# Third quarter's output gates as a Strassen pair inside attention, first value group inside the first long-convolution quarter

## The chip, the cores and the metric

The kernel runs on one core of one Trainium2 chip. The time is the device time of one execution in microseconds; the median over executions is compared. TensorE (PE), VectorE (DVE), ScalarE (ACT), GpSimd (POOL) and SyncE (SP) run side by side; each works through its own list of instructions in order, and semaphores tie the lists together.

## The reference, cut to what matters

One layer of a hybrid network for 640 tokens (128 context tokens and 512 latent tokens), width 1024, in fp32:

```
z = h @ w_in                                   # hy (3 x 1024), g_h, q, k, v, g_a, m
hy = short_conv(hy, conv_w, conv_b)            # 3 taps along the sequence
v_h, x1, x0 = split(hy)
u = v_h * x1
y_h = (irfft(rfft(u) * rfft(filter)) + u * d) * x0      # long convolution
y_a = attention(q, k, v)                       # neighbourhood attention, context keys
p_h = (y_h * silu(g_h)) @ w_bh
p_a = (y_a * silu(g_a)) @ w_ba
out = (sigmoid(m_h) * p_h + sigmoid(m_a) * p_a) @ w_out
x = layer_norm(alpha * x + gate * out)
```

The change concerns two parts of `z`: the output gates `g_h` of the long convolution, `y_h * silu(g_h)`, and the values `v` of attention.

## The kernel before, in words

All products are made of three passes: the operands are split into a high and a low part (`split`: ScalarE rounds the high part, line 112, VectorE subtracts, line 113), and high x high, high x low and low x high are summed. A weight tile is 128 x 1024; a projection (`proj`, matmuls on line 181) takes 8 slices x 3 passes x 2 halves of 320 columns, 48 matmuls. In the convolution quarters the low part of the weights is made by an accumulating transfer on GpSimd (line 161) instead of VectorE.

The kernel goes through these parts:

- A prologue (modulation, filters' hidden layers), with an order written out by hand.
- Four quarters of 256 channels of the long convolution. In quarter `q`, `quarter_head(q + 1)` projects and convolves `u` and `x1` of the next quarter and `quarter_tail(q)` projects `x0`; beside them run `gated_conv(q - 1)`, `long_conv(q)`, `long_conv_back(q)` (Fourier transforms as matmuls, with long chains of elementwise work on VectorE between them) and `filter_spectrum(q + 1)`. The function `weave` interleaves the two lists in the program; the compiler's scheduler then sets the order on every engine.
- `hand_over`, woven with the last quarter's convolution: `quarter_tail(3)`, then the value groups and the first queries and keys (`values(1)`, `values(2)`, `values(3)`, `queries(0)`, `keys(0)`, `values(0)`) with sums of the activations that the pairs below need (`early_sums`). A value group is 120 matmuls of 256 columns (lines 954 and 966) for 256 of the 1024 channels; groups 1 to 3 are stored to DRAM (`v_d`) and read back when attention comes to them (`values_back`). `attention_setup` closes the convolution's memory and opens attention's; `late_sums` make the remaining sums in it.
- Eight main stages of attention, in which TensorE's order is written out by hand: the attention steps of stage `j` (`attend(j)`) are woven into two or three pairs (`mains(j)`). A pair (`pair_tile`, matmuls on line 1229) computes two projection tiles with Strassen's scheme (Winograd's form): 7 products of 4 slices x 3 passes, 84 matmuls of 320 columns instead of 96; VectorE makes four sums of the weights (line 1189) and seven splits for it and combines the products (lines 1238 and 1244). The list `runs` names the order of the pairs, so that `prepare` can sum and split the next pair's weights while the present one runs.
- Output projections, again as plain tiles and pairs, and the layer norm.

The gates of a quarter in `LATE_GATES` are not computed in `quarter_tail`: `x0` alone is, in a compact layout; `gated_conv` stores `x0 * y` to DRAM (`yu_d`), and `gates_h(q)` in a main stage reads it back, computes the gates of both tiles as a pair, multiplies and stores the rows to `yh_d`. For a quarter that isn't listed, `quarter_tail` computes two plain gate tiles (`gate_tile`: one projection, tanh on ScalarE, two products on VectorE, line 571), GpSimd multiplies with `x0` (`gapped_product`), and `gated_conv` stores the finished rows. Before the change this is so for the third quarter (index 2) only. All rows of `yh_d` are read back around the end of the last main stage (`yh_raw`).

The list `GATED_AT` holds sixteen pairs in which, at the fourth product, one row of the output gate's modulation is added up on VectorE (`gate_row`, line 1338; 1024 columns). `EARLY_VALUES` maps a quarter to a value group that is computed at the end of that quarter's list; before the change it is empty. Such a group leaves its accumulators to the tile `dinv` in the convolution's memory, which the short convolution's taps use too. The projections, the values and the pairs share four PSUM banks (`ps_mm`); a projection takes two of them, a value group three.

Of the kernel before, what the change touches and what calls it, by code (L numbers as in the profile page):

```python
# [19 lines left out]
NK = 8  # L20
# [12 lines left out]

T_GH, T_Q, T_K, T_V, T_GA, T_MH, T_MA, T_BH, T_BA, T_WO = 24, 32, 40, 48, 56, 64, 72, 80, 88, 96

LATE_GATES = (0, 1, 3)
EARLY_VALUES = {}

PACKS = (
    (("cc", 16), ("bss", 16), ("sel", 2)),  # L40
# [10 lines left out]
def tile_hyena_natten_step(ctx: ExitStack, tc: tile.TileContext, a, o):  # L51
# [546 lines left out]
    def quarter_tail(q):  # L598
        for i in range(2):
            n = 2 * q + i  # L600
            if q in LATE_GATES:
                x0 = row(yhp, "yh", f"x0_{n}")
# [116 lines left out]
    def gated_conv(q):  # L719
# [7 lines left out]
        for i in range(2):  # L727
# [4 lines left out]
            for j, r in enumerate((0, 2, 1, 3)):  # L732
                nc.tensor.transpose(oy[:, r * P : r * P + P], ye[:, j, i * P : i * P + P], ident)
            if q in LATE_GATES:
                x0, s0 = out["yh"][n], SC
# [11 lines left out]
            for d in range(2):  # L747
                nc.vector.tensor_tensor(ys[:, :, 1:, d], x_rest[:, :, :, d], yo[:, :, :7, d], op=ALU.mult)
            nc.sync.dma_start((yu_d if q in LATE_GATES else yh_d)[n], yh[:])
            yield  # L750

    N_CONV, N_BACK, N_GATED = 10, 7, 2
# [10 lines left out]
    def chain(*gens):  # L763
        for g in gens:
            yield from g
# [56 lines left out]
    def early_sums():  # L822
        t = []
        yield from first_sums(0, t)
        yield from second_sum(0, t[0])
        yield from first_sums(1, t)
        out["early_sums"] = True
# [7 lines left out]
    def alongside(main, side, every, first=0):  # L835
        for i, _ in enumerate(main):
            if i >= first and i % every == 0:
                next(side, None)
            yield
        for _ in side:  # L840
            pass
# [50 lines left out]
    def queries(j):  # L892
        for hf, p in enumerate((yield from proj(T_Q + j, eng="dma", low_last=True))):
            q_half(j, hf, p[:, :HALF])
        yield
# [29 lines left out]
    def keys(j):  # L925
        cached_keys(j)
        for hf, p in enumerate((yield from proj(T_K + j, eng="dma", low_last=True))):
            k_half(j, hf, p[:, :HALF])
        yield

    def values(m):
        w = [wtile(T_V + 2 * m + i, "dma", width=256) for i in range(2)]
        ps = [acc(f"v{m}_{i}") for i in range(2)]
        if m:
            if m in EARLY_VALUES.values():
                v = hwa.tile([P, 1280], F32, tag="dinv", name=f"vs{m}")
                v = [v[:, 512 * i : min(512 * i + 512, 1280)] for i in range(3)]
            else:
                v = [slot(0, t, f"v{m}{t}")[:, :n] for t, n in (("k", 512), ("kl", 768))]
                v = [v[0], v[1][:, :512], v[1][:, 512:]]  # L940
        else:
            out["v0"] = slot(0, "v", "v0")
            v = [out["v0"][:, 512 * i : min(512 * i + 512, 1280)] for i in range(3)]

        def passes(k):
            wh, wl = w[k // 4][0][k % 4], w[k // 4][1][k % 4]
            return ((hH, wh, k == 0, False), (hL, wh, False, False), (hH, wl, False, k == NK - 1))

        for half in range(2):
            ks = range(4 * half, 4 * half + 4)  # L950
            for k in ks:
                for x, wk, first, last in passes(k):
                    for t in range(4):
                        nc.tensor.matmul(  # L954
                            ps[t // 2][:, t % 2 * 256 : t % 2 * 256 + 256], x[:, k, P * t : P * t + P], wk,
                            start=first and t % 2 == 0, stop=last, skip_group_check=True,
                        )
                yield
            if half:
                for i in range(2):  # L960
                    nc.scalar.activation(v[i], ps[i][:], AF.Copy)
            else:
                pe = acc(f"ve{m}")
            for k in ks:
                for x, wk, first, last in passes(k):
                    nc.tensor.matmul(pe[:, :256], x[:, k, P * 4 :], wk, start=first, stop=last, skip_group_check=True)  # L966
            yield
        nc.scalar.activation(v[2], pe[:, :256], AF.Copy)
        nc.sync.dma_start(o["new_v"][:, m * 256 : m * 256 + 256], v[0][:, :256])
        for i in range(3 if m else 0):  # L970
            nc.sync.dma_start(v_d[m][:, 512 * i : min(512 * i + 512, 1280)], v[i])
        yield
# [5 lines left out]
    N_VALUES = 11  # L978

    def early_values(q):  # L980
        if q in EARLY_VALUES:
            yield from values(EARLY_VALUES[q])

# [5 lines left out]
    def hand_over():  # L989
        nonlocal tp  # L990
        yield from quarter_tail(3)
        hwa_stack.close()
        out["slots_l"] = left.enter_context(tc.tile_pool(name="slots_l", bufs=1))
        out["slots_q"] = left.enter_context(tc.tile_pool(name="slots_q", bufs=1))
        tp = left.enter_context(tc.tile_pool(name="tp", bufs=1))
        yield from alongside(chain(values(1), values(2), values(3), queries(0), keys(0), values(0)), early_sums(), 1)

    tail = ctx.enter_context(ExitStack())
    ac = ctx.enter_context(ExitStack())
# [255 lines left out]
    def queries_keys(j):  # L1255
        cached_keys(j)
        yield from pair_tile(T_Q + j, T_K + j, lambda i, hf, src: k_half(j, hf, src, False) if i else q_half(j, hf, src))
# [12 lines left out]
    def gates_h(m):  # L1270
        yu = [row(yhp, "yh", f"yv{m}"), sp.tile([P, NT], F32, tag="yu", name=f"yw{m}")]
        for i in range(2):
            load_to(yu[i][:], yu_d[2 * m + i])

        def use(i, hf, src):
            th = sp.tile([P, HALF], F32, tag="c", bufs=4, name=f"tg{m}")[:]
            y = yu[i][:, CS[hf]]
            nc.scalar.activation(th, src, AF.Tanh, scale=0.5)
            nc.vector.tensor_tensor(y, y, src, op=ALU.mult)
            gate(th, y, y)  # L1280
            nc.scalar.dma_start(yh_d[2 * m + i][:, CS[hf]], y)

        yield from pair_tile(T_GH + 2 * m, T_GH + 2 * m + 1, use)

    def mix(m):
        t0, dst = (T_MH, mh_d) if m < 4 else (T_MA, ma_d)
        n0 = 2 * (m % 4)

        def use(i, hf, src):
            th = sp.tile([P, HALF], F32, tag="c", bufs=4, name=f"th{m}")[:] if hf == i == 0 else src  # L1290
            nc.scalar.activation(th, src, AF.Tanh, scale=0.5)
            nc.scalar.dma_start(dst[n0 + i][:, CS[hf]], th)

        yield from pair_tile(t0 + n0, t0 + n0 + 1, use)

    N_PAIR = 14

    def qk_(j):
        return T_Q + j, T_K + j

    def ga_(j):
        return T_GA + j, T_GA + j + 1

    def gh_(m):
        return T_GH + 2 * m, T_GH + 2 * m + 1

    def mix_(m):
        t = (T_MH if m < 4 else T_MA) + 2 * (m % 4)
        return t, t + 1

    runs = (
        (
            qk_(1), ga_(0), qk_(2), mix_(0), gh_(0), qk_(3), mix_(1), ga_(2), qk_(4), mix_(2), gh_(1), qk_(5), mix_(3), ga_(4), qk_(6), mix_(4), gh_(3), qk_(7), mix_(5), ga_(6), mix_(6), mix_(7),
        ),
    )
    follow = {x: y for run in runs for x, y in zip(run, run[1:])}
    GATED_AT = [runs[0][i][0] for i in (2, 3, 6, 7, 8, 9, 11, 12, 13, 14, 15, 17, 18, 19, 20, 21)]

    weave(hand_over(), chain(gated_conv(2), long_conv(3), long_conv_back(3), gated_conv(3), attention_setup(), late_sums()),
          2 * NK + 3 * N_VALUES + 16, 2 * N_GATED + N_CONV + N_BACK + 7)  # L1320
    gp = left.enter_context(tc.tile_pool(name="gp", bufs=1))
    gbc = gp.tile([P, 2, D], F32, tag="gbc", name="gbc")

# [49 lines left out]
    def last_pair(main):  # L1373
        for i, _ in enumerate(main):
            if i == 0:
                for n in range(2):
                    yh_raw(n)
                    yh_split(n)
            elif i == 5:
                wraw(T_BH)  # L1380
                yh_raw(2)
                yh_raw(3)
                wraw(T_BH + 1)
            yield

    def mains(j):
        return {
            0: ((queries_keys(1), gates_a(0)), 2 * N_PAIR),
            1: ((queries_keys(2), mix(0), gates_h(0)), 3 * N_PAIR),
            2: ((queries_keys(3), mix(1), gates_a(2)), 3 * N_PAIR),  # L1390
            3: ((queries_keys(4), mix(2), gates_h(1)), 3 * N_PAIR),
            4: ((queries_keys(5), mix(3), gates_a(4)), 3 * N_PAIR),
            5: ((queries_keys(6), mix(4), gates_h(3)), 3 * N_PAIR),
            6: ((queries_keys(7), mix(5), gates_a(6)), 3 * N_PAIR),
            7: ((mix(6), last_pair(mix(7))), 2 * N_PAIR),
        }[j]

    with tc.manual_schedule(engines={mybir.EngineType.PE}):
# [400 lines left out]
```

## Time and profile before

| | |
|---|---|
| median of 3 executions | 857.53 us (857.39 to 858.14) |
| profiled execution | 857.72 us |
| its span, first to last instruction | 855.8 us |
| granted TensorE clock, mean | 0.998 |
| TensorE busy | 846.8 us, 6360 matmuls |
| VectorE busy | 710.5 us |
| ScalarE busy | 480.9 us |
| GpSimd busy | 167.3 us |

The profiled execution took 1.9 us more than the span that the profile shows; that part lies before the first and after the last instruction. Busy time of TensorE counts overlapping matmuls once. Matmuls are pipelined: the duration of a single one (309 ns for 320 columns) is longer than the distance to the next.

### The profile page before, as it was taken

To read this page: it belongs to the slowest core of one execution; us is meant where nothing else is said; L and a number is where in the kernel's file an instruction comes from. 1 tells how busy PE (TensorE), PEld (TensorE's weight loads), DVE (VectorE), ACT (ScalarE), POOL (GpSimd) and SP (SyncE) were. 2 spreads that over 40 slices of the span, in tenths; PEclk is the share of its full clock that TensorE was granted. 3 is DMA by queue.
4 is the path that set the end of the run, shared out by engine and by line. 5 is a ranking of instruction groups with operands and counts; after the bars stand their busy time and mean duration, and the time that the engine had idled before them with its cause. 6 is when DMAs were issued, how large, how long until landed. Compare 5 with 4: busy or idle time off the path is not lost.

```text
span 855.8 us, 16832 instructions
## 1 busy us (share of the span) xinstructions
PE 846.8 (99%) x6360; PEld 818.8 (96%) x6360; DVE 710.5 (83%) x1407; ACT 480.9 (56%) x1037; POOL 167.3 (20%) x160
## 2 busy tenths in 40 slices
PE   9999999999999999999999999999999999999996
PEld 7999999999999999999999999999999999999885
DVE  6687697698898866988898989897988778799696
ACT  4575766667665554756565565665665654355310
POOL 0010240231330010521212323232323200000000
PEclk9999999999999999999999999999999999999999
DMA  9996475565554886625535354635363486445631
GB/s 349 350 260 156 105 153 113 136 151 118 144 131 95 222 193 207 194 81 165 175 113 188 100 171 133 199 108 175 106 184 108 127 261 218 161 120 151 223 149 74
DMA packets 59636, 140.48 MB, mean 164 GB/s; under 512 B 8703, under 2 KB 26627, under 8 KB 59556
## 3 DMA queue, kind: packets, MB, share of 16 engines
q1 hardware_dynamic: 47316, 114.70, 40.7%
q0 software_dynamic: 4896, 17.04, 12.3%
q10 hardware_dynamic: 7344, 7.67, 2.6%
q8 instruction: 50, 0.82, 0.4%
q14 instruction: 30, 0.25, 0.1%
HBM read 121.30 MB, written 18.09 MB: 163 GB/s over the span
## 4 chain that ended last, share of the span: by engine, by line
PE 91%; DVE 5%; issue 2%; DMA 1%; ACT 0%; DVEq 0%; POOLq 0%
PE sp L1229 31%; PE mm L181 27%; PE out L1618 6%; PE v L954 5%; PE s L1074 3%; PE pt L1067 3%; PE s L1025 2%; DVE wb L113 2%; PE mm L195 2%; PE ve L966 1%; PE adaT L266 1%; DMA wb<-wall 1%; PE mm L285 1%; DVE s L1189 1%; PE yb L169 1%
## 5 line engine op out<-in xcount | busy, mean ns | idle before, releaser
L1229 PE MATMUL sp<-t,wb 128*128 128x320 f32 x1056 | 166.5, 311 | 0.4 <-DVE wb L113 0.2
L1229 PEld LDWEIGHTS sp<-t,wb 128*128 128x128 f32 x1056 | 156.1, 188 | 3.4 <-DVE wb L113 1.7
L1229 PE MATMUL sp<-hH,wb 128*128 128x320 f32 x528 | 126.5, 311 | 0.0
L112 ACT ACTIVATE wb<-s 128x512 fp32r<-128x512 f32 x104 | 63.4, 629 | 57.0 <-DVE s L1189 22.5
L1229 PEld LDWEIGHTS sp<-hH,wb 128*128 128x128 f32 x528 | 90.5, 188 | 1.6 <-issue 1.6
L181 PE MATMUL mm<-hH,wh 128*128 128x320 f32 x352 | 82.7, 310 | 0.0
L181 PE MATMUL mm<-hL,wh 128*128 128x320 f32 x352 | 82.0, 310 | 0.0
L1229 PE MATMUL sp<-hL,wb 128*128 128x320 f32 x264 | 81.4, 308 | 0.0
L181 PE MATMUL mm<-hH,wl 128*128 128x320 f32 x352 | 81.4, 309 | 0.0
L113 DVE TENSOR_TENSOR wb<-s,wb 128x512 fp32r<-128x512 f32 x104 | 70.8, 693 | 4.6 <-ACT wb L112 4.3
L161 POOL DMA_DIRECT2D wl<-wall x31 | 27.1, 874 | 240.2 <-ACT wl L160 221.6
L112 ACT ACTIVATE wb<-raw 128x512 fp32r<-128x512 f32 x75 | 47.0, 627 | 42.6 <-PE sp L1229 32.2
L1050 POOL TENSOR_SCALAR p<-p,sm 128x384 f32<-128x384 f32 x32 | 44.9, 1414 | 110.5 <-DVE sm L1047 105.5
L181 PEld LDWEIGHTS mm<-hL,wh 128*128 128x128 f32 x352 | 59.2, 188 | 0.5
L181 PEld LDWEIGHTS mm<-hH,wl 128*128 128x128 f32 x352 | 59.0, 188 | 0.5
L181 PEld LDWEIGHTS mm<-hH,wh 128*128 128x128 f32 x352 | 59.2, 188 | 0.2
L113 DVE TENSOR_TENSOR wb<-raw,wb 128x512 fp32r<-128x512 f32 x75 | 52.3, 697 | 6.2 <-ACT wb L112 5.8
L1229 PEld LDWEIGHTS sp<-hL,wb 128*128 128x128 f32 x264 | 49.6, 188 | 0.0
L162 ACT ACTIVATE wh<-raw 128x1024 fp32r<-128x1024 f32 x31 | 32.8, 1058 | 29.0 <-PE mm L181 22.8
L1244 DVE TENSOR_TENSOR c<-sp,u 128x320 f32<-128x320 f32 x78 | 37.6, 482 | 13.0 <-PE sp L1229 12.9
L181 PE MATMUL mm<-yhs,wh 128*128 128x320 f32 x256 | 47.9, 309 | 0.0
L1050 POOL TENSOR_SCALAR edge<-edge,sm 128x320 f32<-128x320 f32 x32 | 46.1, 1449 | 0.2 <-DVE sm L1047 0.2
(408 smaller groups left out, 2145.0 us busy)
## 6 DMA issues: line engine op xcount, KB each, us to landing
raw<-wall SPq DMA_DIRECT2D x93, 512.0 KB, 3.8
wl<-wall POOLq DMA_DIRECT2D x31, 512.0 KB, 5.7
ada<-wada SPq DMA_DIRECT2D x16, 512.0 KB, 9.0
tm<-bias SPq DMA_DIRECT2D x16, 512.0 KB, 5.2
xw<-xw SPq DMA_DIRECT2D x8, 512.0 KB, 8.6
gate<-wgate SPq DMA_DIRECT2D x8, 512.0 KB, 3.7
wo<-wall SPq DMA_DIRECT2D x8, 512.0 KB, 4.5
dec<-decay SPq DMA_DIRECT2D x20, 128.0 KB, 2.7
```

What stands on the lines that cost most here:

```text
L112: hi = nc.scalar.activation(dst_h, src, AF.Copy)
L113: return hi, (eng or nc.vector).tensor_tensor(dst_l, src, f(dst_h), op=ALU.subtract)
L161: nc.gpsimd.dma_start(wl, a["wall"][i], accum_op=ALU.add)
L162: nc.scalar.activation(wh, raw[:], AF.Copy)
L181: nc.tensor.matmul(ps[hf][:, :HALF], wt[k], x[:, hf * HALF : (hf + 1) * HALF], start=(i == 0 and k == 0), stop=(i == lead[2] and k == NK - ...
L954: nc.tensor.matmul(ps[t // 2][:, t % 2 * 256 : t % 2 * 256 + 256], x[:, k, P * t : P * t + P], wk, start=first and t % 2 == 0, stop=last, ...
L1050: nc.gpsimd.tensor_scalar_mul(pv, pv, sm[:, 2, h : h + 1])
L1067: nc.tensor.transpose(pt[:, i * P : i * P + P], x, ident)
L1074: nc.tensor.matmul(dst, lhs, rhs, start=start, stop=stop, skip_group_check=True)
L1229: nc.tensor.matmul(dst, wk, x(xi, k), start=j < 4 and k == 0 and i == 0, stop=k == 3 and i == 2, skip_group_check=True,)
L1244: after = nc.vector.tensor_tensor(c, dst, c if j == 3 else u, op=ALU.add)
L1618: ins = nc.tensor.matmul(dst, x, w[:, w1 : w1 + n], start=i == 0, stop=i == len(steps) - 1, skip_group_check=True)
```

## The change

`LATE_GATES` gets quarter 2, so that all four quarters' gates are pairs in main stages. The fifth main stage's gate pair is now quarter 2's; quarter 3's moves to the start of the last main stage, which has three pairs then. `GATED_AT` is numbered anew: the pairs `qk_(3)` and `gh_(3)` get a gate row, the last two mix pairs lose theirs. `EARLY_VALUES` puts value group 1 at the end of the first quarter's list, and `hand_over` no longer computes it; the divisor of its `weave` follows.

```diff
-LATE_GATES = (0, 1, 3)
-EARLY_VALUES = {}
+LATE_GATES = (0, 1, 2, 3)
+EARLY_VALUES = {0: 1}
...
-        yield from alongside(chain(values(1), values(2), values(3), queries(0), keys(0), values(0)), early_sums(), 1)
+        yield from alongside(chain(values(2), values(3), queries(0), keys(0), values(0)), early_sums(), 1)
...
-            qk_(1), ga_(0), qk_(2), mix_(0), gh_(0), qk_(3), mix_(1), ga_(2), qk_(4), mix_(2), gh_(1), qk_(5), mix_(3), ga_(4), qk_(6), mix_(4), gh_(3), qk_(7), mix_(5), ga_(6), mix_(6), mix_(7),
+            qk_(1), ga_(0), qk_(2), mix_(0), gh_(0), qk_(3), mix_(1), ga_(2), qk_(4), mix_(2), gh_(1), qk_(5), mix_(3), ga_(4), qk_(6), mix_(4), gh_(2), qk_(7), mix_(5), ga_(6), gh_(3), mix_(6), mix_(7),
...
-    GATED_AT = [runs[0][i][0] for i in (2, 3, 6, 7, 8, 9, 11, 12, 13, 14, 15, 17, 18, 19, 20, 21)]
+    GATED_AT = [runs[0][i][0] for i in (2, 3, 5, 6, 7, 8, 9, 11, 12, 13, 14, 15, 17, 18, 19, 20)]
...
-          2 * NK + 3 * N_VALUES + 16, 2 * N_GATED + N_CONV + N_BACK + 7)
+          2 * NK + 2 * N_VALUES + 16, 2 * N_GATED + N_CONV + N_BACK + 7)
...
-            5: ((queries_keys(6), mix(4), gates_h(3)), 3 * N_PAIR),
+            5: ((queries_keys(6), mix(4), gates_h(2)), 3 * N_PAIR),
...
-            7: ((mix(6), last_pair(mix(7))), 2 * N_PAIR),
+            7: ((gates_h(3), mix(6), last_pair(mix(7))), 3 * N_PAIR),
```

The quarters' list that the values join, unchanged by the diff: `chain(quarter_head(q + 1), quarter_tail(q), early_values(q))`.

## Rows read from the trace of the kernel before

**Rows 1.** The page, busy time of each engine.
```profile
PE 846.8 (99%) x6360; PEld 818.8 (96%) x6360; DVE 710.5 (83%) x1407; ACT 480.9 (56%) x1037; POOL 167.3 (20%) x160
```
**Rows 2.** TensorE's waits in the whole run: sum, times, longest, us.
```profile
PE mm L285 <- DVE hid L277: 1.2, 1, 1.2
PE sp L1229 <- DMA wb<-wall: 0.3, 1, 0.3
```
**Rows 3.** Chain that ended last: start us, us, what.
```profile
293.87 5.65 PE v L954 x48
...
417.62 1.50 PE s L1025 x18
...
463.59 1.50 PE s L1025 x18
...
509.86 1.50 PE s L1025 x18
...
685.57 28.16 PE mm L181 x192
```
**Rows 4.** Stretches: length, busy us (count) per engine, clock, DMA share, GB/s.
```profile
98.10:163.30 65.20, 65.20 (x463) 64.76 (x462) 52.11 (x79) 42.98 (x88) 19.68 (x17) 1.00 0.59 134
163.30:224.80 61.50, 61.50 (x439) 61.06 (x438) 55.04 (x81) 41.06 (x77) 19.43 (x18) 1.00 0.58 127
224.80:281.60 56.80, 56.80 (x435) 56.38 (x434) 51.24 (x77) 34.40 (x63) 12.03 (x11) 1.00 0.60 132
281.60:362.10 80.50, 80.50 (x643) 79.63 (x641) 65.09 (x135) 44.03 (x97) 17.08 (x19) 1.00 0.72 204
...
309.80:332.10 22.30, 22.30 (x173) 22.30 (x172) 10.56 (x29) 10.90 (x25) 2.15 (x6) 1.00 0.72 181
332.10:362.10 30.00, 30.00 (x236) 29.13 (x234) 28.00 (x68) 19.72 (x54) 12.34 (x10) 1.00 0.66 212
...
647.70:682.70 35.00, 35.00 (x320) 33.27 (x319) 27.90 (x67) 22.72 (x56) 12.80 (x10) 1.00 0.33 103
```
**Rows 5.** VectorE's work for gate tiles and for pairs, by line.
```profile
L571 DVE SCALAR_TENSOR_TENSOR yh<-yh,mm x4: 469/476/486, 222.4 to 241.9; 128x320 f32<-128x320 f32 x4
...
L1189 DVE TENSOR_TENSOR s<-raw,raw x26: 676/683/693, 322.8 to 773.7; 128x512 f32<-128x512 f32 x26
...
L113 DVE TENSOR_TENSOR wb<-s,wb 128x512 fp32r<-128x512 f32 x104 | 70.8, 693 | 4.6 <-ACT wb L112 4.3
...
L1244 DVE TENSOR_TENSOR c<-sp,u 128x320 f32<-128x320 f32 x78 | 37.6, 482 | 13.0 <-PE sp L1229 12.9
```
**Rows 6.** The gate rows of full length: ns min/median/max, first and last start.
```profile
L1338 DVE SCALAR_TENSOR_TENSOR gbc<-gate,st,gbc x14: 1269/1276/1580, 440.3 to 678.9; 128x1024 f32<-128x1024 f32 x14
```
**Rows 7.** Waits of TensorE's weight loads in attention, 343 to 686 us.
```profile
PEld sp L1229 <- DVE wb L113: 1.7, 5, 0.4
```
**Rows 8.** Loads of the finished rows: issue ns, first and last start.
```profile
L68 SPq DMA_DIRECT2D yhraw<-yh_d x8: 319/327/430, 629.7 to 686.6; - x8
```
**Rows 9.** The value tiles: first matmuls, first eviction.
```profile
L954 PE MATMUL v<-wh,hH x128: 276/279/363, 251.8 to 337.8; 128*128 128x256 f32 x128
...
L961 ACT ACTIVATE v1k<-v x1: 599/599/599, 279.9 to 279.9; 128x512 f32<-128x512 f32 x1
```
**Rows 10.** VectorE's waits from 281.6 to 309.8 and from 309.8 to 332.1 us.
```profile
DVE yh L745 <- PE yp L726: 1.8, 1, 1.8
...
DVE pl L113 <- ACT ph L112: 2.6, 3, 1.5
DVE yu L745 <- PE yp L726: 2.1, 1, 2.1
```
**Rows 11.** Rows of the last quarter leaving (us to landing), who waits, first scores.
```profile
yu_d<-yu SPq DMA_DIRECT2D x6, 320.0 KB, 3.0
...
POOL edge L1013 <- DMA yu_d<-yu: 13.5, 1, 13.5
...
L1025 PE MATMUL s<-k,q x80: 302/328/457, 342.1 to 660.0; 64*128 64x320 f32 x32, 64*128 64x384 f32 x32, 64*128 64x128 f32 x16
```

## The prediction, made before the change was run

> **What bounds the kernel now.** I read the page first, then TensorE's waits, the chain that ended last, busy time by stretch, and the waits of VectorE where the stretches looked tight. The page says that TensorE is the bound: it is busy 846.8 us, 99% of the span [rows 1]. Its waits say that this is no average over unlike stages: in the whole run its longest wait for another engine is 1.2 us, at the very start, and the next is 0.3 us [rows 2]. So the time is, nearly, the sum of the matmuls, and two questions decide: how many matmuls go, and whether some other engine is late when they are gone.
>
> The chain gives the price of a matmul where they follow each other without a break: 192 of 320 columns in 28.16 us, 146.7 ns each; 48 of 256 columns in 5.65 us, 117.7 ns each [rows 3]. The busy time per stretch shows how much VectorE has left beside TensorE: 52.11 of 65.20 us in the first quarter, 55.04 of 61.50 in the second, 51.24 of 56.80 in the third, 65.09 of 80.50 from there into attention, and 28.00 of 30.00 in the last part of that [rows 4]. The granted clock is 1.00 in all these stretches, the 2.4 GHz level; I see nothing in the change that would lower it.
>
> **The change, part by part.**
>
> *Gates of the third quarter.* Out: two plain gate tiles of 8 x 3 x 2 = 48 matmuls each, 96 x 146.7 ns = 14.08 us. In: one pair of 7 x 4 x 3 = 84, 12.32 us. Net -1.76 us, on the engine that sets the end. This is the only term that can shorten anything, and it is 0.2% of the time: about what a measurement of this kernel can tell from no change.
>
> The Trainium skill, "TensorE: Matmul & The Clock Gate", section "Back-to-back issue gap", gives N/2.4 + 2.5 ns for an isolated step, 135.8 ns at N = 320; as an estimate from that page the twelve matmuls would be worth 1.63 us. The trace's 146.7 ns is longer, and is what I use.
>
> Beside TensorE, the two tiles took four VectorE gate products of 0.476 us (1.9 us) [rows 5], GpSimd's products with the short convolution, two weight conversions on ScalarE for each tile and an accumulating GpSimd transfer for each. The short convolution is now written in two parts, so that ScalarE's taps and GpSimd's adds double in number. The quarter keeps its VectorE products; its two rows are stored to another DRAM tensor. I cost all of that at nothing: the second quarter already has just this form, GpSimd was busy 19.43 us there, and TensorE 61.50 of 61.50 us [rows 4].
>
> The pair costs VectorE 4 weight sums (0.68), 7 splits (0.69), 5 combinations (0.48) and 8 gate operations (0.48): 2.7 + 4.9 + 2.4 + 3.9 = 13.9 us, and ScalarE 7 halves and 4 tanh, SP two loads of gate inputs and two of weights, ScalarE's queue four stores [rows 5]. The fifth main stage gets the third quarter's pair in the place of the last quarter's, of the same form: nothing. The last stage gets the extra one. It had VectorE busy 27.90 of 35.00 us [rows 4]; with the pair, and one gate row (1.28 us [rows 6]) instead of two, that is 27.9 + 13.9 - 1.3 = 40.5 us beside 35.0 + 12.3 = 47.3 us of TensorE, 86%, like the stages before it. Its seven attention steps are as many as before, only wider apart. Hidden, as long as the splits run ahead; without that cover a wait costs up to 0.4 us [rows 7].
>
> The last quarter's gated rows are now stored at the start of the last stage. They are read back last: the eight loads of such rows run from 629.7 to 686.6 us, the last after the final pair [rows 8], and two pairs, 24 us, lie between. On SP's queue the pair's four loads move behind those of the last query/key pair, one mix and one gate pair, on ScalarE's queue its stores stand just before those of the two last mix pairs; nobody is waiting for either. Nothing.
>
> *Gate rows.* The long vector operation of 1.28 us moves into the query/key pair of the second stage, and leaves the two final mix pairs. From one stage's first scores to the next the chain shows 417.62, 463.59, 509.86: stages of 45.97 and 46.27 us [rows 3]. The first of these, the one that is to get a row, has none in its query/key pair, the next has one, and TensorE's weight loads waited for splits in five places [rows 7]. So +0.3 us for the second stage; the bounds are 0 and 0.4. The two final pairs give nothing back: no wait stands there.
>
> *The value group.* 120 matmuls of 256 columns, 120 x 117.7 ns = 14.1 us, leave the stretch after the third quarter and stand at the end of the first. With them go two weight loads on SP, two accumulating transfers on GpSimd, four conversions and three evictions on ScalarE, and four stores on SP; on both queues the loads now stand ahead of the second quarter's weights, where the transfer engines were busy 0.59 of the time [rows 4]. TensorE's sum does not change. In the first quarter VectorE, ScalarE and GpSimd were busy 52.11, 42.98 and 19.68 of 65.20 us [rows 4], so their share of it is hidden there, and the quarters' tiles move later by two places. That helps the third quarter: before, this group started at 251.8 us and its result could be moved out only at 279.9 us [rows 9], when memory of the convolution came free, so a second group could hardly have filled in. With the gates gone one group would not have been enough; now the second group takes the first one's place.
>
> But the handover pays. From 281.6 us (the third quarter's output product) to 362.1 us (weights of the second pair in attention), TensorE had 80.5 us of work; now 80.5 - 14.1 = 66.4 us. VectorE has 65.09 us to do in it [rows 4]. Below: 0, if VectorE packs to 98%. Above: its waits there that no order removes. In the trace they are 1.8 us for the third quarter's transposes, 2.6 us for ScalarE's halves, 2.1 us for the last quarter's transposes [rows 10], and 3.0 us until the last output rows have landed, which GpSimd's first clearing in attention waited for [rows 11]: 9.5 us, so 65.1 + 9.5 - 66.4 = 8.2 us. Between them I take 0.4 us, the longest wait for a split in attention [rows 7]: VectorE was idle 80.5 - 65.1 = 15.4 us there, more than the 14.1 us that it must catch up, and idle 11.7 of 22.3 us between 309.8 and 332.1 us [rows 4], mostly for TensorE pieces that stood behind the very filler that is now gone; and it was idle another 5.6 us in the third quarter, less 1.9 us of gate work.
>
> Sum: -1.76 + 0.3 + 0.4 = -1.1 us. The profiled execution took 857.7 us (a span of 855.8 and 1.9 us around it), the median is 857.5; from the median, **856.4 us**.
>
> **Rivals.**
>
> *1. VectorE becomes the bound at the handover (slower).* For it: it was busy 28.00 of 30.00 us from 332.1 to 362.1 us [rows 4], the late sums and the bias tiles can't start before the last quarter's rows have left [rows 11], and TensorE wants attention 14 us earlier. Against it: the idle time counted above. It decides from the point where VectorE's work and unavoidable waits pass 66.4 us: a loss of 2 to 8.2 us on top of -1.5 us, 858 to 864 us, middle 861. The Trainium skill, "Perfetto Trace Analysis", section "Identifying the Most-Contended Engine", says to take the engine of highest occupancy as the one to improve, and for VectorE occupancy is the fair measure; by that rule this stretch would be VectorE's after the change (98% by the rows above), and this rival's time would follow. The trace of before agrees only for its last 30 us.
>
> *2. The value group stalls the first quarter (slower).* Its accumulators take three of the four banks that the projections share, and its result goes to the scratch tile that the short convolution's taps use. For it: before, such a result waited from the end of its matmuls to 279.9 us for its memory [rows 9]. Against it: the taps are done soon in that quarter. Price: one group's matmuls at most, 14.1 us, more likely 2 to 5: 858 to 861 us.
>
> *3. All hidden, and the small waits go too (faster).* The five waits for splits are 1.7 us in sum [rows 7]; if the later order removes half of them instead of adding one: 857.5 - 1.8 - 0.9 = 854.9 us.
>
> *4. The order doesn't change.* TensorE's order in the quarters is chosen by the compiler's scheduler; it may put the value group late again. Then the filler is where it was and the gain stays: 855.8 to 856.4 us.
>
> **How the numbers follow.** Forecast case 0.48 (its own range 855.6 to 857.4), rival 1 0.30, rival 2 0.08, rival 3 0.09, rival 4 0.05. The bound of 0.2%, 1.7 us, lies at 855.8 and 859.2 us. Faster: rival 3, and a fifth of the forecast case: 0.19. Slower: rival 2 with most of its weight and the part of rival 1 above 859.2: 0.32. The rest, 0.49, is no change. The range leaves out half of rival 3 and the upper end of rivals 1 and 2: 855.3 to 862.0 us.
>
> **What would show it.** Right: 6348 matmuls instead of 6360; stretches of the second and third quarter with TensorE fully busy; first scores in attention some 14 us earlier than 342.1 us [rows 11]; the second stage 0.3 us longer; TensorE's waits still under 3 us. Wrong: a wait of TensorE for VectorE's splits, sums or bias work within 40 us after the first scores (rival 1), or one around 110 to 140 us (rival 2).

## The result and the profile after

The changed kernel takes 864.74 us (median of 6 runs, 864.23 to 866.46); the kernel before, run beside it, 857.93 us (857.39 to 858.53). The ratio is 1.0082, with a 95% interval of 1.0071 to 1.0092: slower by 6.8 us. 856.4 us was predicted, with 862.0 us as the upper end of the range. The profiled execution took 864.72 us, of which the span is 862.9 us.

The page's busy times, which answer to [rows 1]:

```profile
PE 848.1 (98%) x6348; PEld 819.1 (95%) x6348; DVE 720.0 (83%) x1427; ACT 482.5 (56%) x1047; POOL 166.0 (19%) x156
```

Twelve matmuls fewer, as the change says. TensorE's waits in the whole run, against [rows 2] (sum, times, longest):

```profile
PE sp L1229 <- ACT t L112: 4.2, 1, 4.2
PE mm L285 <- DVE hid L277: 1.2, 1, 1.2
PE adaT L266 <- DMA ada<-wada: 0.7, 2, 0.4
...
PE sp L1229 <- DVE t L113: 0.4, 1, 0.4
```

There is one new long wait, of a pair's product for an operand `t`, a Strassen sum; with the 0.4 us for the sum's other part that is 4.6 us. (Some expectations below count the same wait at the weight loads, where it is 5.3 us.) The stretches of [rows 4], and the neighbourhood of that wait (columns as there):

```profile
98.10:163.30 65.20, 65.16 (x485) 64.47 (x484) 54.49 (x85) 38.43 (x75) 18.32 (x15) 1.00 0.62 145
163.30:224.80 61.50, 61.50 (x438) 61.13 (x437) 49.92 (x75) 40.93 (x84) 17.00 (x15) 1.00 0.59 130
224.80:281.60 56.80, 56.55 (x428) 55.80 (x428) 46.58 (x73) 35.80 (x69) 14.63 (x14) 1.00 0.54 126
281.60:362.10 80.50, 75.83 (x567) 74.20 (x566) 75.08 (x148) 45.36 (x100) 15.22 (x18) 0.96 0.62 182
332.00:337.00 5.00, 0.77 (x3) 0.29 (x1) 4.75 (x17) 4.07 (x14) 2.25 (x3) 0.82 0.98 378
337.00:343.00 6.00, 5.56 (x24) 5.49 (x24) 5.93 (x10) 1.26 (x2) 3.86 (x4) 0.58 0.65 210
```

The quarters are nearly as full as before (the third has 0.25 us idle). In the handover TensorE stands still for 4.2 us of 332 to 337, and from 337 to 343 it does 24 matmuls in 5.56 us, 232 ns each and not 146.7: the granted clock is 0.58 there, so most of that stretch is at the 1.2 GHz level. At 146.7 ns the 24 would take 3.5 us, so the slow stretch costs 2.0 us on top of the wait. The chain that ended last names what the product waited for (start, us, what):

```profile
327.87 1.77 PE sp L1229 x12
...
332.77 0.19 DVE again_t L775
...
333.42 0.49 DVE edge L1040
...
333.95 0.66 ACT edge L1045 x2
334.60 0.60 ACT p L1045 x2
335.20 0.55 ACT edge L1045 x2
335.74 0.65 ACT t L112
...
336.41 1.06 DVE t L113
...
337.51 7.41 PE sp L1229 x35
```

The first pair's first product is done at 329.6 us. Its second reads the sum `t2`, whose second half is one of the three late sums. Between the additions that make it (`again_t`) and its high and low parts (`t`) stands, on both engines, the softmax of attention's first blocks (`edge`, `p`). The first and the last step of the late sums, in the kernel before and then in the changed one (ns min/median/max, first and last start):

```profile
L113 DVE TENSOR_TENSOR t<-again_t,t x3: 820/827/926, 335.9 to 348.0; 128x640 fp32r<-128x640 f32 x3
L791 DVE TENSOR_TENSOR again_t<-t,t x2: 818/818/818, 332.1 to 341.3; 128x640 f32<-128x640 f32 x2
```

```profile
L113 DVE TENSOR_TENSOR t<-again_t,t x3: 812/824/1046, 336.4 to 345.0; 128x640 fp32r<-128x640 f32 x3
L791 DVE TENSOR_TENSOR again_t<-t,t x2: 812/816/821, 330.5 to 341.4; 128x640 f32<-128x640 f32 x2
```

Before, the late sums began at 332.1 us, 10.0 us ahead of the first scores (342.1). Now they begin at 330.5 us, 0.9 us behind the first scores (329.6): TensorE comes 12.5 us earlier, the sums 1.6 us. Lastly attention's clock: all scores, and the chain at the stages' first scores, against [rows 3, 11]:

```profile
L1025 PE MATMUL s<-k,q x80: 302/328/456, 329.6 to 658.5; 64*128 64x320 f32 x32, 64*128 64x384 f32 x32, 64*128 64x128 f32 x16
```

```profile
412.19 1.50 PE s L1025 x18
...
458.45 1.50 PE s L1025 x18
```

From these rows the 7.1 us by which the span grew (862.9 - 855.8) fall into four parts. Up to the first scores: 329.6 against 342.1, -12.5 us, where the 14.1 us of gates went. First scores to 412.19, against to 417.62 before: 82.6 - 75.5 = +7.1 us; this holds the wait and the slow matmuls. The second stage: 46.26 - 45.97 = +0.3 us. From there to the end: 404.45 - 392.21 = +12.2 us, the added pair.

### The profile page after: what moved, and what is told of

It reads as the page before. It is cut to its first block, busy times and chain, and to the rows that moved or that the text cites. A ratio compares the mean times of both kernels' runs of the same rounds, so it can differ in the third digit from the quotient of the medians.

```text
span 862.9 us, 16835 instructions
## 1 busy us (share of the span) xinstructions
PE 848.1 (98%) x6348; PEld 819.1 (95%) x6348; DVE 720.0 (83%) x1427; ACT 482.5 (56%) x1047; POOL 166.0 (19%) x156
## 4 chain that ended last, share of the span: by engine, by line
PE 88%; DVE 6%; issue 2%; DMA 2%; ACT 1%; SPq 0%; DVEq 0%; POOLq 0%; ACTq 0%
PE sp L1229 34%; PE mm L181 23%; PE out L1618 6%; PE v L954 5%; PE pt L1067 3%; PE s L1074 3%; PE s L1025 2%; DVE wb L113 2%; PE mm L195 2%; PE ve L966 1%; DMA ada<-wada 1%; DMA wb<-wall 1%; PE adaT L266 1%; PE yb L169 1%; PE yb L170 1%
## 5 line engine op out<-in xcount | busy, mean ns | idle before, releaser
L1229 PE MATMUL sp<-t,wb 128*128 128x320 f32 x1104 | 176.6, 313 | 4.9 <-ACT t L112 4.2
L1229 PEld LDWEIGHTS sp<-t,wb 128*128 128x128 f32 x1104 | 165.4, 190 | 8.5 <-ACT t L112 4.5
L1229 PE MATMUL sp<-hH,wb 128*128 128x320 f32 x552 | 132.1, 311 | 0.0
L1229 PEld LDWEIGHTS sp<-hH,wb 128*128 128x128 f32 x552 | 94.5, 188 | 1.7 <-issue 1.7
L181 PE MATMUL mm<-hL,wh 128*128 128x320 f32 x320 | 75.1, 310 | 0.0
L181 PE MATMUL mm<-hH,wh 128*128 128x320 f32 x320 | 75.1, 310 | 0.0
L181 PE MATMUL mm<-hH,wl 128*128 128x320 f32 x320 | 74.4, 310 | 0.0
L181 PEld LDWEIGHTS mm<-hL,wh 128*128 128x128 f32 x320 | 54.0, 188 | 0.5
L181 PEld LDWEIGHTS mm<-hH,wl 128*128 128x128 f32 x320 | 53.6, 188 | 0.5
L181 PEld LDWEIGHTS mm<-hH,wh 128*128 128x128 f32 x320 | 53.8, 188 | 0.2
```

Of the source, the lines that this page charges most:

```text
L181: nc.tensor.matmul(ps[hf][:, :HALF], wt[k], x[:, hf * HALF : (hf + 1) * HALF], start=(i == 0 and k == 0), stop=(i == lead[2] and k == NK - ...
L1229: nc.tensor.matmul(dst, wk, x(xi, k), start=j < 4 and k == 0 and i == 0, stop=k == 3 and i == 2, skip_group_check=True,)
```

## The experiments

Each ratio is to the kernel before, run on the same chip beside it; the changed kernel's own is 1.0082. Each edit also lets the compiler's scheduler set the order of VectorE's and ScalarE's queues anew; where the traces show that it changed, the text says so. "Handover" is the stretch from the third quarter's output product to the end of the first pairs in attention.

**One half of the change at a time.** Gates alone:

```diff
-EARLY_VALUES = {0: 1}
+EARLY_VALUES = {}
-chain(values(2), values(3), queries(0), ...)
+chain(values(1), values(2), values(3), queries(0), ...)
```

> The gates half of the change alone: the value group stays in the handover. Theory A (with the third quarter's gates gone, TensorE has 14.1 us less to do before attention, VectorE hardly less, so the first attention pair waits for its late sums wherever a value group stands; after the change that wait is 4.4 + 0.9 us and the slow matmuls behind it cost some 2.4 us): as slow as the changed kernel or slower, 864 to 870 us, a wait over 3 us either in the first attention pair or in the third quarter. Rival V (the value group in the first quarter is what costs): the gates' twelve matmuls are won, 855.5 to 856.5 us.

871.83 us, ratio 1.0167 (1.0152 to 1.0183). Theory A holds, in a form worse than expected: 1.8 us above its range. TensorE's waits and stretches:

```profile
PE fp L169 <- ACT sh L112: 3.6, 1, 3.6
PE v L954 <- ACT v1k L961: 2.6, 1, 2.6
```

```profile
270.00:276.00 6.00, 2.20 (x11) 1.82 (x10) 5.56 (x15) 2.84 (x7) 0.00 (x0) 0.83 0.00 0
276.00:282.00 6.00, 5.47 (x27) 5.11 (x25) 5.97 (x18) 1.73 (x4) 0.00 (x0) 0.60 0.28 111
```

The hole is now at the end of the third quarter, where the gates were: 3.6 us before a Fourier product (`fp`) and then 2.6 us before a value group, which waits until the one ahead of it has been moved out (`v1k`). Again the clock falls behind the waits. The value group in the first quarter does not make the hole; it moves it to the handover, and makes it smaller.

The value group alone:

```diff
-EARLY_VALUES = {}
+EARLY_VALUES = {0: 1}
-chain(values(1), values(2), values(3), queries(0), ...)
+chain(values(2), values(3), queries(0), ...)
```

> The other half alone: value group 1 in the first quarter, all gates as in the kernel before. Theory A: TensorE's work ahead of attention is the same as before, so no wait of the first attention pair, first scores at about 342 us, 857 to 858.5 us. Rival V: most of the loss is here, 862 to 866 us.

860.0 us, ratio 1.0023 (1.0013 to 1.0034): neither. There is no wait for the late sums, but some 2 us are lost. First scores are at 344.5 us; the third quarter, which had no idle time [rows 4], is short of matmuls:

```profile
224.80:281.60 56.80, 55.74 (x397) 54.86 (x395) 47.25 (x67) 36.02 (x67) 17.38 (x16) 1.00 0.55 122
```

**Order in attention.** The first two scores' tiles later:

```diff
-weave(chain(*main), attend(j), n_main, ..., 1 if j < 7 else 0)
+weave(chain(*main), attend(j), n_main, ..., (5, 1, 1, 1, 1, 1, 1, 0)[j])
```

> The changed kernel, but the first two blocks of scores are written four half products later in the first attention stage, behind the second and third product of the pair, so that their softmax (some 4 us on VectorE, 4 us on ScalarE between 331.9 and 337 us) no longer stands between the late sums. Theory A: the pair's wait falls from 5.3 us to 2 to 4 us, and with it the time at the low clock: 860 to 863.5 us. Rival V: the wait is only a symptom and shows up elsewhere, 864 to 865 us.

867.85 us, 1.0115 (1.0100 to 1.0130): missed. The wait for `t` is still 4.0 us, since the sum comes 1.9 us earlier (334.6 and not 336.4 us) but TensorE does too, by the scores that it skips; and two waits of 0.9 us for the next weights join it, behind the softmax that now comes later.

Needless matmuls in the place of the wait:

```diff
+if i0 == T_Q + 1 and j == 1 and k == 2:
+    for _ in range(30): nc.tensor.matmul(ps["v"], wb[1][:, 0, :P], ...)
```

> The changed kernel with 30 needless matmuls of 320 columns (4.4 us at 146.7 ns, their results overwritten) just before the matmuls that wait for the late sum. If the granted clock of 0.58 from 337 to 343 us comes from TensorE's standing still before it, the clock stays at 1.00 and the time falls by 2 to 3 us, to 861.7 to 862.7 us, although nothing is ready earlier. If the clock has another cause: 864.2 to 865.2 us, and clock low in the same place.

869.45 us, 1.0137 (1.0120 to 1.0154). Half right: stretches and waits of that run,

```profile
332.00:337.00 5.00, 4.82 (x33) 4.52 (x31) 4.75 (x17) 4.17 (x14) 2.38 (x3) 1.00 1.02 405
337.00:343.00 6.00, 5.52 (x37) 5.33 (x39) 5.96 (x11) 2.01 (x3) 3.83 (x4) 1.00 0.56 191
...
350.50:355.00 4.50, 4.50 (x18) 4.50 (x19) 3.42 (x7) 1.18 (x4) 4.50 (x2) 0.50 0.62 246
```

```profile
PE sp L1233 <- DVE t L113: 3.5, 2, 2.9
PE sp L1233 <- ACT t L112: 1.8, 1, 1.8
```

With TensorE kept busy the clock is 1.00 from 337 to 343 us, and 37 matmuls fit where 24 did: the fall came from standing still. But TensorE then waits for the sixth product's sum, 1.8 and 2.9 us, and the clock falls there (0.50, 18 matmuls in 4.5 us, 250 ns each). TensorE comes to it earlier, and the sum comes later:

```profile
L113 DVE TENSOR_TENSOR t<-again_t,t x3: 808/814/1045, 336.4 to 349.4; 128x640 fp32r<-128x640 f32 x3
```

Its last step starts at 349.4 us, behind the softmax of the next two blocks; in the changed kernel it stood ahead of that, at 345.0. The edit changed VectorE's order, so the run shows what the clock does, and its time does not show what filling alone is worth.

**VectorE's load.** Fourteen low halves of weights on GpSimd, on the changed kernel and, as a control, on the kernel before:

```diff
-split(wb[j][:, 0], wb[j][:, 1], src[j])
+split(wb[j][:, 0], wb[j][:, 1], src[j], nc.gpsimd if i0 in (T_Q + 1, T_GA) else None)
```

> The changed kernel with the low halves of the weights of the first two pairs in attention (14 subtractions of 0.69 us on VectorE, 9.7 us) made by GpSimd. Theory A2 (VectorE has more to do in the handover than TensorE leaves room for; an order only moves the wait, and work taken off VectorE takes it away): of the 8 us lost in waits and low clock at least 4 go, 857 to 861 us. Rival C (the late sums are late because their scratch memory comes free only when the last output rows have landed, at 330.4 us, and VectorE's load does not matter): 863.5 to 865.5 us. Rival G (GpSimd is too slow for it, its nearest row is 1.78 us for 128x512): slower than 865.5 us, with TensorE waiting for GpSimd's halves.

> Control: the kernel before with the same 14 low halves on GpSimd. There TensorE does not wait at the handover, so theory A2 expects no gain from it, 857 to 858.3 us; rival G expects a loss here too, over 859 us.

875.71 us, 1.0211 (1.0194 to 1.0228), and 866.22 us, 1.0100 (1.0085 to 1.0115): by these times rival G, on both. Its sign, TensorE waiting for GpSimd, is there in the control alone; in the changed kernel TensorE waits for the sums, 4.3 us and later 7.3 us. The control, then the changed kernel with the edit:

```profile
PE sp L1229 <- POOL wb L113: 4.9, 2, 2.6
```

```profile
PE sp L1229 <- ACT t L112: 11.6, 2, 7.3
```

And VectorE is slowed meanwhile. The same two small operations, first in the changed kernel, then in this run while GpSimd's subtractions (1.3 to 1.8 us each) stand beside them:

```profile
L923 DVE TENSOR_TENSOR kl<-ck,k x2: 284/286/289, 332.3 to 332.5; 128x128 fp32r<-128x128 f32 x2
```

```profile
L923 DVE TENSOR_TENSOR kl<-ck,k x2: 1344/1344/1344, 332.4 to 333.6; 128x128 fp32r<-128x128 f32 x2
```

So these two say nothing about VectorE's load, which leaving the same work out does:

```diff
-wl = wb[j][:, 1, ...]
+wl = wh if i0 in (T_Q + 1, T_GA) else wb[j][:, 1, ...]   # and no split on VectorE
```

> The changed kernel, and for the first two pairs in attention the low halves of the weights are left out: TensorE reads the high half in their place, with as many matmuls, and VectorE does 14 subtractions of 0.69 us (9.7 us) less, with nothing given to GpSimd. Theory A2: the loss at the handover shrinks by 4 us or more, waits there under 2 us in sum, 857 to 860.5 us. Theory O: the first wait stays at 3 us or more, 861 to 865 us.

867.95 us, 1.0112 (1.0096 to 1.0128). That is above both ranges. VectorE now has idle time (7.51 of 10 us busy), and TensorE waits all the same, 3.1 us in the second product and 3.1 us in the sixth:

```profile
330.00:340.00 10.00, 6.87 (x43) 6.13 (x40) 7.51 (x21) 7.12 (x18) 5.32 (x6) 0.85 0.94 349
```

```profile
PE sp L1231 <- DVE t L113: 4.2, 2, 2.3
PE sp L1231 <- ACT t L112: 2.0, 2, 1.2
```

```profile
L113 DVE TENSOR_TENSOR t<-again_t,t x3: 818/821/979, 334.9 to 347.6; 128x640 fp32r<-128x640 f32 x3
```

Theory A2 falls: less volume does not help in the order that the scheduler then makes. The second half of `t2` again stands behind the softmax, and the last step of the sixth product's sum, at 347.6 us, now stands behind the softmax of the next blocks too.

**The late sums themselves.** Left out:

```diff
-t = again("t1", 1); ...; yield from third_sum(0, again("t2", 0))
+tok["t2"][i][1] = tok["t3"][i][1]; tok["t4"][i][r] = tok["t1"][i][r]
```

> The changed kernel with the three late sums left out: the pairs read earlier sums in their place, as many matmuls of the same shape; VectorE does 11 operations of 0.82 us less, ScalarE three of 0.73 us. It bounds what hangs on them: if the whole loss is the wait for these sums and the low clock behind it, 856 to 858 us, no wait over 1 us in the first pair and clock 1.00 throughout; if VectorE is late with the weights or the softmax anyway, over 860 us, with a wait for those.

858.81 us, 1.0020 (1.0009 to 1.0031), single runs from 858.25 to 862.11: between the two ranges. The handover's loss goes with the sums: clock 1.00, and 1.1 us of waits, for weights. That VectorE has 9.0 us less to do does not by itself explain it: 9.7 us less, in the order of the run above, won nothing. The other terms account for the rest, -1.76 (gates) + 0.3 (gate row) + 1.6 (ahead of attention) + 1.1 = +1.2 us, against 1.1 us measured.

```profile
330.00:340.00 10.00, 10.00 (x78) 9.37 (x77) 8.17 (x28) 7.30 (x21) 3.69 (x6) 1.00 0.95 351
```

Another sum late in the place of `t2`'s, alone, with the low halves on GpSimd, and with the softmax behind the sums:

```diff
-SUMS = ("t1", "t3", "t2", "t4")
+SUMS = ("t1", "t2", "t3", "t4")   # first_sums(1) makes t2; late_sums makes t3
```

> The changed kernel with another sum left for the end: of the second four rows, the sum that the pair's second product reads is made before the convolution's memory is given back, and the one that the third product reads after it; one more addition of 0.82 us in all, and the need 12 matmuls (1.76 us) later. Rival C (memory that comes free late is the cause): the first wait falls by 1.8 us or more, 860 to 862.5 us. Theory A2: VectorE's work is the same, so the wait moves to the third product or to the sixth, 863.5 to 867 us.

> Both edits: the low halves of two pairs on GpSimd, and the third product's sum late. Theory A2: as with the first edit alone or up to 2 us better, 856 to 860 us. Rival C: as with the second edit alone.

> The third product's sum left for the end instead of the second's, then first the half of the sixth product's sum that is read first, and the softmax of the first two blocks behind all three. Theory O: every sum then comes within about 2 us of its need, 857.5 to 861 us. Theory A2: 863 us or more.

872.87 us (1.0174, 1.0159 to 1.0190), 875.85 us (1.0210, 1.0195 to 1.0225) and 871.97 us (1.0160, 1.0143 to 1.0177). All worse than the changed kernel, and the first two beyond every range given. In the first, TensorE waits 4.7 us in the third product and 5.0 us in the sixth; in the last, 3.1 us for a sum and 6.8 us for PSUM that the late softmax still holds. The same softmax order without the exchange:

```diff
+if j == 0 and b < 2: behind(ins, out["late_end"])   # both reductions of blocks 0 and 1
```

> The changed kernel with one thing fixed in VectorE's order: the softmax of the first two blocks comes after the last of the three late sums; the scores stay where they are on TensorE. Theory O (each late sum is a chain of some 4 us through VectorE and ScalarE that can only begin when the last output rows have landed at 330.4 us; what counts is what stands between its links): the first wait falls from 5.3 to 2 to 3.5 us, the low clock after it shortens, and there is no second wait over 2 us, 859.5 to 862.5 us. Theory A2 (the volume of VectorE's work counts, not its order): the wait moves to the sixth product or to the first transposes, 863.5 to 867 us.

868.13 us, 1.0120 (1.0105 to 1.0135). The first wait shrinks as theory O says (2.4 us), but the time is above both ranges, since the next scores wait for the banks that the softmax was to free:

```profile
PE s L1025 <- DVE sm L1040: 3.5, 1, 3.5
PE sp L1233 <- ACT t L112: 2.4, 1, 2.4
```

**The memory under them.**

```diff
-yh = hw.tile([P, ROW], F32, tag="u", ...)[:, :NT] if q == 3 else ...
+yh = slot(1, ("q", "ql")[i], f"yu{n}")[:] if q == 3 else ...
```

> The changed kernel, with one memory address moved: the last quarter's two output rows are built in the slots that the second pair of heads' queries get later, not in the convolution's memory, so that this memory comes free when VectorE has read it (about 326 us) and not when the rows have landed (329 to 330 us). Not an operation more or less. Theory C (what makes the late sums late is that their memory comes free late): they start 3 to 5 us earlier, the waits of 5.3 us shrink to under 2.5 us, 859 to 862 us. Rival O2 (the sums' chain through VectorE's and ScalarE's queues is too long wherever it starts): less than 1.5 us is won, 863.2 to 866 us.

> Control: the kernel before with the same rows elsewhere. TensorE does not wait for the late sums there, so by theory C nothing changes, 857 to 858.5 us; if the edit by itself were worth something, under 856.5 us.

> The rows elsewhere, and the third product's sum left for the end instead of the second's. Theory C: the first wait goes wholly, one of up to 2 us may stay at the sixth product, 857.5 to 861 us. Rival O2: 866 us or more, as without the rows elsewhere (872.9 us).

864.65 us (1.0086, 1.0071 to 1.0101), the control 857.31 us (1.0000, 0.9990 to 1.0009), and 871.49 us (1.0167, 1.0152 to 1.0183). Theory C falls as a cause by itself: with the rows elsewhere the sums start at 330.3 us, not at 330.5, because VectorE, without a gap from 317 us on, comes to them in its queue only then.

```profile
L791 DVE TENSOR_TENSOR again_t<-t,t x2: 808/811/814, 330.3 to 341.1; 128x640 f32<-128x640 f32 x2
```

The value group in the second quarter (`EARLY_VALUES = {1: 1}`), with the rows elsewhere:

> The rows elsewhere, and the value group at the end of the second quarter's list instead of the first's. The handover is that of the run with the rows elsewhere. If the 1.6 us lost ahead of attention come from the value group standing in the first quarter, up to 1.5 us less than that run; if they come from the third quarter's lacking the gates' matmuls, the same within 0.7 us.

878.95 us, 1.0244 (1.0227 to 1.0261): worse than anything expected. TensorE waits 3.6 us behind the third quarter and 7.6 us for a late sum; which part of the order did this was not followed up.

**Order, memory and load together.** The edit in short, with `behind` standing for a dependency that puts the first in a queue after the second:

```diff
+behind(softmax of blocks 0 and 1, last of the sum "t4" 0); behind(blocks 2 and 3, last of "t4" 1)
+behind(wb[3:6] of the first pair, last of "t2" 1); late sums in the order t2, t4 0, t4 1
+scores of blocks 2 and 3 after half product 14
```

> Several edits of order together on the changed kernel, no operation more or less: the last rows elsewhere, the second product's sum ahead of the first pair's fourth and later weights, then the sixth product's two sums with the half that is read first in front, the softmax of the first two blocks behind that half, and the next two blocks' scores only after the first pair. Worked out from durations of the changed kernel's trace: the second product's sum is ready at about 331.9 us, when TensorE wants it (no wait), the sixth's about 2.4 us late. If VectorE's in-order queue holds several things that are due at once, and each single edit only let the next one come last (theory Q): one wait of 2 to 3 us and a shorter stretch at the low clock, 859.5 to 862 us. If the order has no part in it: 864 us or more.

> The same order and memory, and the low halves of the first two pairs' weights left out as in the run with the low halves out (TensorE reads the high half instead; VectorE does 9.7 us less). By theory Q volume counts once the order is right: the sixth product's sum comes by 337 us, before TensorE wants it at 338.1 us, no wait over 1 us, clock 1.00, 857 to 859 us. If volume never counts: as without the leaving out, over 859.5 us.

Order and memory: 866.16 us, 1.0094 (1.0077 to 1.0111), a miss. The first wait is 1.9 us, but the sixth product waits another 1.8 us, because its sum stands on ScalarE behind the copy of a weight whose buffer TensorE had yet to free, and 2.4 us are a later wait for weights. TensorE's waits, then ScalarE's:

```profile
PE sp L1244 <- ACT t L119: 2.9, 2, 1.9
PE sp L1244 <- DVE wb L120: 2.4, 1, 2.4
```

```profile
ACT wb L119 <- PE sp L1244: 6.6, 1, 6.6
```

With the low halves left out on top: 859.88 us, 1.0024 (1.0015 to 1.0034), 6.3 us less. Theory Q's signs are there, no wait over 1 us in the handover and clock 1.00, but the time is 0.9 us above its bound and just inside the other case's "over 859.5":

```profile
PE sp L1248 <- ACT t L119: 0.8, 1, 0.8
PE sp L1248 <- ACT wb L1214: 0.8, 1, 0.8
```

```profile
330.00:340.00 10.00, 8.73 (x58) 7.81 (x55) 9.16 (x17) 5.68 (x13) 0.00 (x0) 1.00 0.91 344
```

ScalarE's order changed with it. Its copies of the late sums, in the run with order and memory and then in this one:

```profile
L119 ACT ACTIVATE t<-again_t x3: 724/728/736, 333.5 to 344.3; 128x640 fp32r<-128x640 f32 x3
```

```profile
L119 ACT ACTIVATE t<-again_t x3: 723/736/741, 331.5 to 337.7; 128x640 fp32r<-128x640 f32 x3
```

The last of them starts 6.6 us earlier, and none stands behind a weight's copy that waits for TensorE. The same 9.7 us taken from VectorE won nothing in the order as scheduled and came with 6.3 us in this one; how much of that is the load and how much ScalarE's queue, these runs don't separate.

## Why the prediction was wrong

*The gates, -1.76 us: right.* 6348 matmuls; the added pair costs 12.2 us from the second stage's end on, against 12.32, with no wait added in the last stage.

*The gate row, +0.3 us: right.* The second stage went from 45.97 to 46.26 us.

*The value group, nothing: too low.* The first quarter hid it (65.16 of 65.20 us of TensorE), but attention begins 12.5 and not 14.1 us earlier. By itself the move costs about 2 us (ratio 1.0023). The third quarter shows where a part is: 1.06 us idle in that run, 0.25 us in the changed kernel. 0.7 us are waits for weight transfers in the opening, which are 0.2 to 0.7 us in most of these runs and can't be put down to the change. The rest of the 1.6 us is not settled.

*The handover, +0.4 us: the step that failed.* It cost 7.1 us: 4.2 and 0.4 us of waits, 2.0 us of slow matmuls, and 0.5 us in smaller pieces. The interval from 0 to 8.2 us held, in part by luck, since 2.0 us of the cost are slow matmuls that its working did not have; the choice in it was wrong. I took the low end because VectorE had been idle for 15.4 us there and had 14.1 to catch up. That counts idle time as if it could be spent anywhere. The chain and the runs show why it can't: attention's first pair needs three late sums, each a chain of additions on VectorE, a copy on ScalarE and a subtraction on VectorE. Before, they began 10.0 us ahead of the first scores; now 0.9 us behind them. They stand in two in-order queues among the last quarter's products, the next weights and the first softmax, in an order that was fixed when the program was built. Without the sums the loss is gone (858.81 us); VectorE's load, the memory and the place of the softmax, changed one at a time, each with the order that the scheduler then makes, leave it or move it to the next result that is due; order, memory and load together bring it down to 859.88 us.

*The low clock: not in the sum.* I wrote that nothing in the change would lower it. Nothing did directly; the wait did. The filled run shows it: with TensorE busy through the wait, the clock was 1.00 from 337 to 343 us and not 0.58.

*Rival 1 was what happened.* Its sign, a wait for VectorE's sums within 40 us of the first scores, came 2.6 us after them. Its loss of 2 to 8.2 us takes in the 7.1 us measured; its time, 858 to 864 us, was passed by 0.7 us because of the 1.6 us ahead of attention. The range, up to 862.0 us, had left out its upper end. Its mechanism, VectorE as the bound, is true only in part. The Trainium skill, "Perfetto Trace Analysis", section "Identifying the Most-Contended Engine", would have the engine of highest occupancy relieved first. VectorE was at 75.08 of 80.5 us, but relief alone won nothing; a gain came only with the changed order, and there ScalarE's queue has a share in it.

*Rivals 2, 3 and 4:* no wait at 110 to 140 us, no gain, and the order did change.

What stays open: whether an order exists that recovers the loss with all the work done (the one tried, 866.16 us, lost 1.8 us behind a copy on ScalarE and 2.4 us for weights), and what shares order, memory and load have in the last run. No version here beats the kernel before.

## What to carry to other kernels

Matmuls that need little of the other engines are filler, and what they are worth is the slack that they give to whoever is late behind them. Before moving such work, list what is due at its old place, result by result with the queue it stands in and the time it is wanted; a sum of idle time only bounds the loss. Price a wait of TensorE as the wait and the slow matmuls after it (here 4.6 us and 2.0 us), and when a single remedy only moves the wait, try the remedies together before giving up one of them.

## What the hardware showed unexpectedly

After a wait of 4.2 us the granted clock was 0.58 over the next 6 us, 232 ns for a matmul of 320 columns; after waits of 1.8 and 2.9 us in the filled run, 0.50 over 4.5 us, 250 ns. A shorter wait did not always bring a shorter slow stretch: in the run with order and memory the clock was 0.58 over 6 us too, after waits of 1.9 and 0.2 us.

```profile
336.00:342.00 6.00, 6.00 (x27) 6.00 (x26) 5.42 (x9) 0.00 (x0) 0.00 (x0) 0.58 0.71 252
```

In the run without the late sums and in the one with order, memory and load, where no wait of the handover passed 0.8 us, it stayed at 1.00.

A subtraction of 128x128 on VectorE took 1344 ns and not 286 while GpSimd worked on 128x512 beside it. The Trainium skill, "SBUF — State Buffer", section "SBUF: two separate sides", has the two engines share one pair of ports, which an operation with two inputs in SBUF holds as a whole; these operations have two, and the trace agrees: 1344 ns is about what one of GpSimd's takes there (1.3 to 1.8 us).
